# mLSTM normalisers carried as rows, state stores on the scalar queue, and the RWKV inverse's masks in fp16 on VectorE

## The chip, the cores and the metric

The kernel runs on one core of one Trainium2 chip. The time is what the device takes for one execution, in microseconds (us). Before the change three executions took 1936.51 us in the median (1935.79 to 1941.13).

## The reference, cut to what matters

One inference step of a two-layer hybrid network on 384 tokens: 128 context tokens and 256 latent ones, model width 1024. Layer 0 mixes with Mamba-2 SSD heads beside 16 RWKV-7 heads, layer 1 with 4 GLA heads beside 4 mLSTM heads; each layer ends in a squared-ReLU MLP. Every mixer scans the tokens in both directions, starts the latent scan from a given state and returns the context's final state. Two pieces matter here. The RWKV-7 scan is, per head and direction,

```
S_t = S_{t-1} (diag(w_t) - kk_t (kk_t * a_t)^T) + v_t k_t^T,   y_t = S_t r_t
```

and the mLSTM scan keeps beside its matrix C (128 x 256 per head and direction) a normaliser n, a vector of 128:

```
C_t = f_t C_{t-1} + i_t v_t k_t^T,   n_t = f_t n_{t-1} + i_t k_t
h_t = (C_t q_t) / max(|n_t . q_t|, exp(-m_t))
```

Inputs hold n as `state_mlstm_n` (2 directions x 4 heads x 128), outputs return it as `new_mn` in the same shape.

## The kernel before, in words

The work runs through four parts: the mixer of layer 0 ("ab"), its MLP, the mixer of layer 1 ("cd"), its MLP. All big products take a weight from memory (`raw`), split it into a high part `wH` (ScalarE, L265) and a low part `wL` (mostly VectorE, L223), and multiply three times on TensorE (`dps`). In the two mixers these products are the filler beside the scans. Python generators give the steps of each scan and of the filler, `run` takes them in turn by step counts, and the tile framework's scheduler then fixes one static order for each engine. Each engine works through its list in order, so an instruction that waits holds all behind it.

**The RWKV inverse** (`rw_inverse`, from L1210). The scan goes in chunks of 64 tokens; a strictly triangular matrix A per head and chunk (six chunks, two heads on the two halves of the partitions, in `Q`) has to be inverted. There are 16 such inverses, one per pair of heads and direction, one in each round of part "ab". An inverse starts from a mask of A for blocks of 1 (`AO`), and then doubles the block size in five levels, m = 2 to 32: a masked copy of A (`AOb`, block diagonal over the two heads, two buffers) meets the inverse so far (`pz`), the product is copied to `Zb` by ScalarE, two more products (`pw2`, `pt2`) update `W` and `Tm` on VectorE. Before, the masked copies of the five levels are made by GpSimd straight from `Q` (fp32) and a bf16 mask, one multiplication for each head's half. ScalarE also writes `AHb`, an fp16 copy of A in the same block-diagonal layout; its off-diagonal blocks were set to zero once. It is used at the end of the inverse only, together with the rest `ALb`.

**mLSTM** (`ml_core`, from L2268; one call per head, spread over two rounds of part "cd"). It loads C and n of both directions side by side into `CN` (n is column 256), one DMA for C and one of 128 x 1 elements per direction for n. The context's final state is a product of 257 columns in PSUM, copied to `mso` by ScalarE, and stored by two DMAs from SyncE's queue, 128 x 256 for C (L2307) and 128 x 1 for n (L2308). SyncE's queue (SP) also issues every weight load. `gla_core` stores its final states the same way (L2208), and `cd_setup` the stabiliser `new_mm` (L2091).

Of the kernel before, what the change touches and what calls it, by code (L numbers as in the profile page):

```python
# [8 lines left out]
F32 = mybir.dt.float32  # L9
F32R = mybir.dt.float32r  # L10
BF16 = mybir.dt.bfloat16
F16 = mybir.dt.float16
U32 = mybir.dt.uint32
AF = mybir.ActivationFunctionType
ALU = mybir.AluOpType
# [148 lines left out]
class Net:  # L164
# [793 lines left out]
    def rw_setup(self):  # L958
        nc = self.nc
        rp = self.rp  # L960
        i64 = rp.tile([128, 64], F16, name="i64h")
        nc.vector.tensor_copy(i64, self.c("i64"))
        self.i64h = i64
        self.i128h = rp.tile([128, 128], F16, name="i128h")
        nc.vector.tensor_copy(self.i128h, self.c("ident"))
        a, b = GOFF["rw"]
        nm = COFF["r64"][1]
        self.rwmask = rp.tile([128, nm], BF16, name="rwmask")
        self.r64 = rp.tile([128, b - a - nm], F32, name="r64")
        with self.tc.tile_pool(name="rwc", bufs=1) as pp:  # L970
            t = pp.tile([128, nm], F32, name="rwc")
            nc.sync.dma_start(out=t, in_=self.I["const"][:, a:a + nm])
            nc.vector.tensor_copy(self.rwmask, t)
        nc.sync.dma_start(out=self.r64, in_=self.I["const"][:, a + nm:b])
        self.pads = []
        for i in range(1):
            t = rp.tile([128, 387], F32, name="rpad%d" % i)
            nc.gpsimd.memset(t, 0.0)
            self.pads.append(t)
        self.npad = 0  # L980
        self.mu_om = rp.tile([128, 27], F32, name="mu_om")
        self.mu_h = rp.tile([128, 27], F32, name="mu_h")
        self.ts(self.mu_om, self.par("rwkv_mu"), -1.0, ALU.mult, 1.0, ALU.add)
        self.ts(self.mu_h, self.par("rwkv_mu"), 0.5, ALU.mult)
        self.hw0 = rp.tile([128, 16], F32, name="hw0")
        self.ha0 = rp.tile([128, 16], F32, name="ha0")
        self.ts(self.hw0, self.par("rwkv_w0"), -1.0, ALU.mult)
        self.ts(self.ha0, self.par("rwkv_a0"), -1.0, ALU.mult)

        self.bks = rp.tile([128, 2, 2, 8], F32, name="bks")  # L990
        for e, h in enumerate((slice(0, 64), slice(64, 128))):
            nc.gpsimd.memset(self.bks[h, e, 0], 1.0)
            nc.gpsimd.memset(self.bks[h, e, 1], 0.0)
            ka = self.par("rwkv_k_a")[h]
            nc.vector.tensor_copy(self.bks[h, 1 - e, 0], ka)
            self.ts(self.bks[h, 1 - e, 1], ka, -1.0, ALU.mult, 1.0, ALU.add)
        self.wdt = rp.tile([128, T], F32, name="wdt")
        self.adt = rp.tile([128, T], F32, name="adt")
        self.gdt = rp.tile([128, T], F32, name="gdt")
# [208 lines left out]
    def rw_inverse(self, d, st):  # L1208

        nc = self.nc
        rp = self.rpi
        dn = "fb"[d]
        halves = (slice(0, 64), slice(64, 128))
        A = [st["Q"][h, e, :, 0, :] for e, h in enumerate(halves)]
        i64 = self.c("i64")
        f = lambda ap: ap.rearrange("p c t -> p (c t)")  # L1220
        b6 = lambda ap: ap.unsqueeze(1).to_broadcast([ap.shape[0], 6, 64])
        h6 = lambda nm, bufs: rp.tile([128, 6, 64], F16, tag=nm, name=nm, bufs=bufs)

        def heads(name, lhs, rhs):
            p = self.psi(name)
            for c in range(6):
                for h in halves:
                    self.mm(p[h, 64 * c:64 * c + 64], lhs[h, c, :] if lhs.shape[1] == 6 else lhs[h, :],
                            rhs[h, c, :] if rhs.shape[1] == 6 else rhs[h, :])
            return p[:, :T]  # L1230

        def pairs(name, lhs, rhs):
            p = self.psi(name)
            for c in range(6):
                self.mm(p[:, 64 * c:64 * c + 64], lhs[:, c, :], rhs[:, c, :])
            return p[:, :T]

        AO = h6("AO", 1)
        for h, a in zip(halves, A):
            self.tt(AO[h], a, b6(self.rm("rwl1_" + dn)[h]), ALU.mult)  # L1240
        W = h6("W", 2)
        self.tt(W, b6(i64), AO, ALU.subtract)
        yield
        pt = heads("pt", W, self.i64h)
        Tm = h6("T", 2)
        self.acopy(f(Tm), pt)
        for h, a in zip(halves, A):
            self.acopy(self.AHb[h, :, h], a)
        yield
        for n, m in enumerate((2, 4, 8, 16, 32)):  # L1250
            AOb = self.AOb[n % 2]
            for h, a in zip(halves, A):
                self.tt(AOb[h, :, h], a, b6(self.rm("rwl%d_%s" % (m, dn))[h]), ALU.mult, eng=nc.gpsimd)
            pz = pairs("pz", AOb, Tm)
            Zb = self.Zb
            zv = pz.rearrange("p (c t) -> p c t", c=6)
            for h in halves:
                self.acopy(Zb[h, :, h], zv[h])
            yield
            if m < 32:  # L1260
                pw = pairs("pw2", Zb, W)
            pt = self.psi("pt2")
            for c in range(6):
                for h in halves:
                    self.mm(pt[h, 64 * c:64 * c + 64], W[h, c, :], Zb[h, c, h])
            T2 = h6("T", 2)
            if m < 32:
                W2 = h6("W", 2)
                self.tt(f(W2), f(W), pw, ALU.subtract)
                W = W2  # L1270
            self.tt(f(T2), f(Tm), pt[:, :T], ALU.subtract)
            Tm = T2
            if n == 0:
                for h, a in zip(halves, A):
                    self.tt(self.ALb[h, :, h], a, self.AHb[h, :, h], ALU.subtract)
            yield

        pe = self.psi("pe")
        self.mm(pe[:, :T], self.i128h, f(Tm), stop=False)
        for c in range(6):  # L1280
            self.mm(pe[:, 64 * c:64 * c + 64], self.AHb[:, c, :], Tm[:, c, :], start=False, stop=False)
            self.mm(pe[:, 64 * c:64 * c + 64], self.ALb[:, c, :], Tm[:, c, :], start=False, stop=c == 5)
        pt = heads("pt", Tm, self.i64h)
        E = h6("AO", 1)
        self.tt(E, b6(i64), pe[:, :T].rearrange("p (c t) -> p c t", c=6), ALU.subtract)
        W = h6("W", 2)
        self.acopy(f(W), pt)
        yield
        pc = heads("pc", E, W)
        WF = self.rpc.tile([128, 6, 64], F32, tag="WF", name="WF", bufs=2)  # L1290
        self.tt(f(WF), f(W), pc, ALU.add)
        yield
        st["W"] = WF
# [698 lines left out]
    def cd_setup(self, es, hs):  # L1992
# [25 lines left out]
        for d in range(2):  # L2018
            nc.sync.dma_start(out=gbias[32 * d:32 * d + 4, :], in_=I["mlstm_i_b"][0, d].rearrange("(h o) -> h o", o=1))
            nc.sync.dma_start(out=gbias[64 + 32 * d:68 + 32 * d, :], in_=I["mlstm_f_b"][0, d].rearrange("(h o) -> h o", o=1))  # L2020
            nc.sync.dma_start(out=m0[32 * d:32 * d + 4, :], in_=I["state_mlstm_m"][0, 0, d].rearrange("(h o) -> h o", o=1))
        self.Ms = p.tile([128, T], F32R, name="Ms")
        self.ct = p.tile([128, 3, 64], F32, name="mct")
        self.emt = p.tile([128, 3, 64], F32, name="memt")
        self.wit = p.tile([128, 2, 64], F32, name="mwit")
# [4 lines left out]
        def evac(ps):  # L2030
# [57 lines left out]
                V.tensor_copy(f(self.wit), p2[:, 0:128])  # L2088
                self.ts(self.wst, p2[:, 128:192], 128.0 ** -0.5, ALU.mult)
            for d in range(2):  # L2090
                nc.sync.dma_start(out=self.O["new_mm"][0, 0, d].rearrange("(h o) -> h o", o=1), in_=self.mfin[32 * d:32 * d + 4, :])  # L2091
        second = self.dense_cm(W, 0, hs, evac, placed=(6176, 4, 32))
        return [first, second]

# [23 lines left out]
    def gla_core(self, h, u, ys):  # L2118
# [72 lines left out]
        for i, (n, d) in enumerate(((0, 0), (0, 1), (1, 0), (2, 1))):  # L2191
# [13 lines left out]
            if n == 0:  # L2205
                so = tl("gso", [128, 256], 2)
                self.acopy(so, ps[:, :256])
                nc.sync.dma_start(out=self.O["new_gla"][0, 0, d, h], in_=so)  # L2208
            else:
                self.stt(S1[:, d], S0[:, d], gl[:, d:d + 1], ps[:, :256], ALU.mult, ALU.add)  # L2210
            yield
# [60 lines left out]
    def ml_core(self, h, u, ys):  # L2272
# [7 lines left out]
        tks = [slice(128 * n, 128 * n + 128) for n in range(3)]  # L2280
        CN = tl("CN", [128, 2, 257])
        nc.sync.dma_start(out=CN[:, :, 0:256], in_=self.I["state_mlstm_c"][0, 0, :, h].rearrange("d k v -> k d v"))
        for d in range(2):
            nc.sync.dma_start(out=CN[:, d, 256:257], in_=self.I["state_mlstm_n"][0, 0, d, h].rearrange("(k o) -> k o", o=1))

        Gs = tl("Gs", [128, 5, 128])
        blocks = ((1, 2), (0, 0), (1, 1), (2, 2), (2, 1))
# [12 lines left out]
        for d in range(2):  # L2300
            kw = tl("kw", [128, 128], 2)
            self.act(kw, pt[:, :128], AF.Copy, scale=self.wst[:, 32 * d + h:32 * d + h + 1])
            ps = u["ps"]()
            self.mm(ps[:, :257], kw, v[:, 0])
            so = tl("mso", [128, 257], 2)
            self.acopy(so, ps[:, :257])
            nc.sync.dma_start(out=self.O["new_mc"][0, 0, d, h], in_=so[:, 0:256])  # L2307
            nc.sync.dma_start(out=self.O["new_mn"][0, 0, d, h].rearrange("(k o) -> k o", o=1), in_=so[:, 256:257])  # L2308
            yield
        for d in range(2):  # L2310
            r = 32 * d + h
# [161 lines left out]
```

## Time and profile before

| | |
|---|---|
| median of three executions | 1936.51 us |
| the profiled execution | 1942.11 us |
| its span, first to last instruction | 1940.0 us |
| TensorE busy | 1811.7 us (93%) |
| VectorE busy | 1346.5 us (69%) |
| ScalarE busy | 1062.5 us (55%) |
| GpSimd busy | 413.0 us (21%) |
| mean granted TensorE clock | 0.953 of full |

PE stands for TensorE, PEld for its weight loads, DVE for VectorE, ACT for ScalarE, POOL for GpSimd, SP for SyncE; a q behind a name is that engine's instruction queue. A busy time is the union of the instructions' spans. A waiting time is put down to what ended it last. The granted clock is the share of full speed that the chip allowed TensorE in a stretch. Part "ab" lies from about 60 to 980 us in the span, its 16 inverses from 122 to 850 us; part "cd" runs from 1200 to 1660 us, its rounds of heads from 1256 to 1620 us.

### The profile page before, as it was taken

To read this page: it belongs to the slowest core of one execution; us is meant where nothing else is said; L and a number is where in the kernel's file an instruction comes from. 1 tells how busy PE (TensorE), PEld (TensorE's weight loads), DVE (VectorE), ACT (ScalarE), POOL (GpSimd) and SP (SyncE) were. 2 spreads that over 40 slices of the span, in tenths; PEclk is the share of its full clock that TensorE was granted. 3 is DMA by queue.
4 is the path that set the end of the run, shared out by engine and by line. 5 is a ranking of instruction groups with operands and counts; after the bars stand their busy time and mean duration, and the time that the engine had idled before them with its cause. 6 is when DMAs were issued, how large, how long until landed. Compare 5 with 4: busy or idle time off the path is not lost.

```text
span 1940.0 us, 37528 instructions
## 1 busy us (share of the span) xinstructions
PE 1811.7 (93%) x13651; PEld 1510.4 (78%) x13651; DVE 1346.5 (69%) x2890; ACT 1062.5 (55%) x2670; POOL 413.0 (21%) x455
## 2 busy tenths in 40 slices
PE   7879998999999999999899999899998988899998
PEld 3676666766666676876899998598988888799887
DVE  3696788888787886767766334675976867766434
ACT  3557464746564666544555332476776756555322
POOL 2244323242434143421100002011201112200000
PEclk9889999999899897999999999799999999899999
DMA  8422343333333322336344643344434234244432
GB/s 268 119 73 71 102 128 91 97 94 116 96 106 117 86 52 64 91 118 180 87 120 127 204 129 92 102 114 88 94 98 90 80 87 125 87 120 128 146 129 87
DMA packets 322525, 213.57 MB, mean 110 GB/s; under 512 B 41936, under 2 KB 307958, under 8 KB 322340
## 3 DMA queue, kind: packets, MB, share of 16 engines
q1 hardware_dynamic: 319508, 210.45, 38.6%
q8 instruction: 107, 1.75, 0.4%
q10 hardware_dynamic: 2480, 0.59, 0.2%
q14 instruction: 78, 0.64, 0.1%
q0 software_dynamic: 352, 0.13, 0.0%
HBM read 201.32 MB, written 9.78 MB: 109 GB/s over the span
## 4 chain that ended last, share of the span: by engine, by line
PE 70%; DVE 14%; DMA 6%; ACT 5%; issue 3%; POOL 1%; SPq 1%; DVEq 0%; ACTq 0%; POOLq 0%
PE dps L209 43%; PE o L209 7%; PE ps L209 4%; PE mod L209 3%; DVE wL L223 3%; PE aux L209 2%; DMA raw<-in_w_in_cd 2%; DVE cacc L230 2%; PE psc L209 2%; DMA raw<-in_w_mod 1%; PE py L209 1%; PE pt L209 1%; PE pr L209 1%; ACT wH L265 1%; PE pu L209 1%
## 5 line engine op out<-in xcount | busy, mean ns | idle before, releaser
L265 ACT ACTIVATE wH<-raw 128x256 fp32r<-128x256 f32 (+1 forms) x788 | 363.6, 481 | 477.3 <-PE dps L209 344.3
L223 DVE TENSOR_TENSOR wL<-raw,wH 128x256 fp32r<-128x256 f32 (+2 forms) x769 | 424.6, 570 | 270.8 <-ACT wH L265 262.6
L223 POOL TENSOR_TENSOR AO<-Q,rwmask 64x384 f16<-64x384 f32 x160 | 164.4, 1031 | 257.7 <-PE pz L209 185.4
L265 ACT ACTIVATE Zb<-pz 64x384 f16<-64x384 f32 x160 | 77.2, 483 | 41.0 <-PE pz L209 38.5
L230 DVE SCALAR_TENSOR_TENSOR cacc<-rows,params,cacc 128x192 f32<-128x192 f32 (+1 forms) x192 | 96.5, 504 | 0.8
L209 PE MATMUL dps<-sH,wH 128*128 128x384 f32 x232 | 87.7, 379 | 4.9 <-DVE m L223 4.4
L209 PE MATMUL dps<-sH,wL 128*128 128x384 f32 x232 | 81.6, 352 | 0.4 <-DVE wL L223 0.3
L209 PE MATMUL dps<-sL,wH 128*128 128x384 f32 x232 | 81.5, 352 | 0.3 <-DVE sL L223 0.3
L209 PE MATMUL dps<-h0H,wH 128*128 128x384 f32 (+2 forms) x150 | 61.4, 413 | 18.4 <-ACT h0H L233 7.8
L223 POOL TENSOR_TENSOR gDb<-gb 128x384 f32<-128x384 f32 x28 | 32.1, 1147 | 149.4 <-DVE gb L2145 81.0
L209 PE MATMUL mod<-xT,cond 128*32 128x384 f32 (+1 forms) x320 | 55.5, 514 | 8.4 <-DVE Q L223 3.7
L209 PE MATMUL dps<-h0L,wH 128*128 128x384 f32 (+2 forms) x150 | 55.5, 370 | 3.5 <-DVE h0L L230 3.5
L209 PE MATMUL dps<-h6H,wH 128*128 128x384 f32 (+2 forms) x150 | 56.0, 375 | 2.9 <-ACT wH L265 2.7
L209 PE MATMUL dps<-h4H,wH 128*128 128x384 f32 (+2 forms) x150 | 56.2, 380 | 2.1 <-ACT h4H L233 2.1
L209 PE MATMUL dps<-h2H,wH 128*128 128x384 f32 (+2 forms) x150 | 58.1, 387 | 0.0
L209 PEld LDWEIGHTS dps<-h0H,wH 128*128 128x128 f32 (+1 forms) x150 | 29.1, 196 | 33.9 <-ACT h0H L233 9.4
L209 PE MATMUL dps<-h1L,wH 128*128 128x384 f32 (+2 forms) x150 | 55.2, 368 | 0.0
L209 PE MATMUL dps<-h0H,wL 128*128 128x384 f32 (+2 forms) x150 | 55.1, 367 | 0.0
L209 PE MATMUL dps<-h1H,wH 128*128 128x384 f32 (+2 forms) x150 | 54.1, 362 | 0.0
L209 PE MATMUL dps<-h1H,wL 128*128 128x384 f32 (+2 forms) x150 | 53.7, 358 | 0.0
L209 PEld LDWEIGHTS dps<-sH,wH 128*128 128x128 f32 x232 | 45.3, 195 | 10.0 <-issue 5.1
L209 PE MATMUL dps<-h2L,wH 128*128 128x384 f32 (+2 forms) x150 | 53.0, 353 | 0.0
(1112 smaller groups left out, 5614.3 us busy)
## 6 DMA issues: line engine op xcount, KB each, us to landing
raw<-in_w_mlp_up SPq DMA_DIRECT2D x64, 512.0 KB
raw<-in_w_mlp_down SPq DMA_DIRECT2D x64, 512.0 KB
raw<-in_w_in_ab SPq DMA_DIRECT2D x204, 128.0 KB
xT<-in_w_mod SPq DMA_DIRECT2D x128, 192.0 KB
raw<-in_w_in_cd SPq DMA_DIRECT2D x192, 128.0 KB
raw<-in_w_mod SPq DMA_DIRECT2D x64, 192.0 KB
raw<-in_w_mod SPq DMA_DIRECT2D x32, 256.0 KB
raw<-in_w_out_cd SPq DMA_DIRECT2D x64, 128.0 KB
```

What stands on the lines that cost most here:

```text
L209: self.nc.tensor.matmul(out, lhsT, rhs, start=start, stop=stop)
L223: (eng or self.nc.vector).tensor_tensor(out=out, in0=a, in1=b, op=op)
L230: self.nc.vector.scalar_tensor_tensor(out=out, in0=a, scalar=s, in1=b, op0=op0, op1=op1)
L265: self.nc.scalar.activation(out=out, in_=in_, func=AF.Copy)
```

## The change

Three things are changed.

In the inverse the mask tile becomes fp16. ScalarE's copy `AHb` moves to the start, and the masks are applied to it: a VectorE multiplication per half for `AO`, and one VectorE multiplication over all 128 partitions and both heads' columns (768 elements) for each level, `off(n)`. The zero blocks of `AHb` keep the result block diagonal. Masks for levels 0 and 1 are made ahead of the first level, the others two levels ahead.

The normalisers are loaded once, as 8 rows of 128, in `cd_setup`, turned by one TensorE transposition and kept in `mn`; `ml_core` copies its column into `CN` on VectorE. The final ones are gathered in `mno` by VectorE, turned once after the last head, copied and stored as 8 rows. `mso` shrinks by a column, and the last head's `ml_core` has one step more.

The stores of final states in part "cd" (`new_mm`, `new_gla`, `new_mc`, `new_mn`) go out from ScalarE's queue.

```diff
-        self.rwmask = rp.tile([128, nm], BF16, name="rwmask")
+        self.rwmask = rp.tile([128, nm], F16, name="rwmask")
...
+        for h, a in zip(halves, A):
+            self.acopy(self.AHb[h, :, h], a)
+
+        def off(n):
+
+            two = lambda ap: ap.rearrange("p c (e t) -> p c e t", e=2)
+            self.tt(two(self.AOb[n % 2]), two(self.AHb),
+                    self.rm("rwl%d_%s" % (2 << n, dn)).unsqueeze(1).unsqueeze(1).to_broadcast([128, 6, 2, 64]), ALU.mult)
         AO = h6("AO", 1)
-        for h, a in zip(halves, A):
-            self.tt(AO[h], a, b6(self.rm("rwl1_" + dn)[h]), ALU.mult)
+        for h in halves:
+            self.tt(AO[h], self.AHb[h, :, h], b6(self.rm("rwl1_" + dn)[h]), ALU.mult)
         W = h6("W", 2)
         self.tt(W, b6(i64), AO, ALU.subtract)
+        off(0)
         yield
...
-        for h, a in zip(halves, A):
-            self.acopy(self.AHb[h, :, h], a)
+        off(1)
         yield
         for n, m in enumerate((2, 4, 8, 16, 32)):
-            AOb = self.AOb[n % 2]
-            for h, a in zip(halves, A):
-                self.tt(AOb[h, :, h], a, b6(self.rm("rwl%d_%s" % (m, dn))[h]), ALU.mult, eng=nc.gpsimd)
-            pz = pairs("pz", AOb, Tm)
+            pz = pairs("pz", self.AOb[n % 2], Tm)
...
             Tm = T2
+            if n < 3:
+                off(n + 2)
...
+        self.mn = p.tile([128, 2, 4], F32, name="mn")
+        self.mno = p.tile([128, 2, 4], F32, name="mno")
+        t = self.mpool.tile([128, T], F32, tag="nt", name="mnr", bufs=2)[0:8, 0:128]
+        nc.sync.dma_start(out=t, in_=I["state_mlstm_n"][0, 0].rearrange("d h k -> (d h) k"))
+        pn = self.psp("mn")
+        self.tr(pn[:, 0:8], t)
+        V.tensor_copy(self.mn.rearrange("p d h -> p (d h)"), pn[:, 0:8])
...
-                nc.sync.dma_start(out=self.O["new_mm"][0, 0, d].rearrange("(h o) -> h o", o=1), in_=self.mfin[32 * d:32 * d + 4, :])
+                nc.scalar.dma_start(out=self.O["new_mm"][0, 0, d].rearrange("(h o) -> h o", o=1), in_=self.mfin[32 * d:32 * d + 4, :])
...
-                nc.sync.dma_start(out=self.O["new_gla"][0, 0, d, h], in_=so)
+                nc.scalar.dma_start(out=self.O["new_gla"][0, 0, d, h], in_=so)
...
-        for d in range(2):
-            nc.sync.dma_start(out=CN[:, d, 256:257], in_=self.I["state_mlstm_n"][0, 0, d, h].rearrange("(k o) -> k o", o=1))
+        V.tensor_copy(CN[:, :, 256], self.mn[:, :, h])
...
-            so = tl("mso", [128, 257], 2)
-            self.acopy(so, ps[:, :257])
-            nc.sync.dma_start(out=self.O["new_mc"][0, 0, d, h], in_=so[:, 0:256])
-            nc.sync.dma_start(out=self.O["new_mn"][0, 0, d, h].rearrange("(k o) -> k o", o=1), in_=so[:, 256:257])
+            so = tl("mso", [128, 256], 2)
+            self.acopy(so, ps[:, :256])
+            V.tensor_copy(self.mno[:, d, h:h + 1], ps[:, 256:257])
+            nc.scalar.dma_start(out=self.O["new_mc"][0, 0, d, h], in_=so)
+            yield
+        if h == 3:
+            pt = u["ps"]()
+            self.tr(pt[0:8, 0:128], self.mno.rearrange("p d h -> p (d h)"))
+            so = tl("mso", [128, 256], 2)[0:8, 0:128]
+            self.acopy(so, pt[0:8, 0:128])
+            nc.scalar.dma_start(out=self.O["new_mn"][0, 0].rearrange("d h k -> (d h) k"), in_=so)
             yield
```

How the change moves instructions is seen at three places. The first is VectorE's list at the start of the second inverse, before:

```order
L223 TENSOR_TENSOR AO<-Q,rwmask 64x384 x2
L223 TENSOR_TENSOR ALb<-Q,AHb 64x6x64
L223 TENSOR_TENSOR W<-const_base,AO 128x384
L1123 SCALAR_TENSOR_TENSOR b<-r_759,lw 128x384
L227 TENSOR_SCALAR UV<-pu 64x2x64
L223 TENSOR_TENSOR lw<-b,lw 128x384
```

and the same place now:

```order
L223 TENSOR_TENSOR AO<-AHb,rwmask 64x384 x2
L223 TENSOR_TENSOR AO_793<-AHb,rwmask 128x768
L223 TENSOR_TENSOR W<-const_base,AO 128x384
L223 TENSOR_TENSOR AO_795<-AHb,rwmask 128x768
L223 TENSOR_TENSOR ALb<-Q,AHb 64x6x64
L227 TENSOR_SCALAR UV<-pu 64x2x64
L1123 SCALAR_TENSOR_TENSOR b<-r_759,lw 128x384
L223 TENSOR_TENSOR lw<-b,lw 128x384
```

AO_793 and AO_795 are the two buffers `AOb`. Every inverse has five such new instructions, and the first of its masks reads ScalarE's copy where it read VectorE's own `Q`.

The second place is SyncE's list where the first mLSTM head's final state is stored, before:

```order
L664 DMA raw<-in_w_in_cd 128x256 x8
L2307 DMA out_new_mc<-mso 128x256
L2308 DMA out_new_mn<-mso 128x1
L664 DMA raw<-in_w_in_cd 128x2x128 x3
L2307 DMA out_new_mc<-mso 128x256
L2308 DMA out_new_mn<-mso 128x1
L664 DMA raw<-in_w_in_cd 128x2x128 x8
L2208 DMA out_new_gla<-gso 128x256
```

In the changed kernel only the weight loads are left there, and ScalarE's list at that place reads:

```order
L265 ACTIVATE mso<-ps 128x256
L265 ACTIVATE wH<-raw 128x256
L2322 DMA out_new_mc<-mso 128x256
L233 ACTIVATE kw<-ps,mwst 128x128
L265 ACTIVATE wH<-raw 128x256
L233 ACTIVATE gE<-gDf 128x96x2 x2
```

The C store follows its copy by one instruction, and the n store is gone from all lists until the last head.

The third place is ScalarE's list at the start of part "cd", between the MLP's residual and the first normalised tile h0H, before:

```order
L233 ACTIVATE rr<-rr 128x384
L265 ACTIVATE wH<-raw 128x256 x2
L233 ACTIVATE r_16437<-sx,const_base 128x384
L233 ACTIVATE r_16437<-r_16437 128x384
L233 ACTIVATE h0H<-nh,modv_105 128x128
L233 ACTIVATE h0H<-nh,modv_105 128x256
```

and now:

```order
L233 ACTIVATE rr<-rr 128x384
L265 ACTIVATE wH<-raw 128x256 x2
L265 ACTIVATE modsb<-mod 128x384
L233 ACTIVATE r_16364<-sx,const_base 128x384
L233 ACTIVATE r_16364<-r_16364 128x384
L265 ACTIVATE wH<-raw 128x256
L233 ACTIVATE h0H<-nh,modv_105 128x128
```

`modsb` is the copy of the last modulation product `mod`, which reads weights from memory; before it stood behind h5H. On VectorE and TensorE the modulation's end has moved ahead in the same way (TensorE: all 32 pieces of `mod`, then the new transposition `mn`, then the first `dps`).

## Rows read from the trace of the kernel before

**Rows 1.** The page: the chain that ended last, by engine, shares of the span.

```profile
PE 70%; DVE 14%; DMA 6%; ACT 5%; issue 3%; POOL 1%; SPq 1%; DVEq 0%; ACTq 0%; POOLq 0%
```

**Rows 2.** Windows by stage: length, busy us (instructions) per engine, PEclk, DMA share, GB/s.

```profile
122.00:850.00 728.00, 680.95 (x7286) 496.22 (x7286) 585.21 (x1288) 428.13 (x1087) 263.82 (x266) 0.94 0.33 93
1243.00:1625.00 382.00, 358.51 (x2178) 336.71 (x2178) 278.56 (x627) 252.39 (x733) 50.00 (x66) 0.97 0.41 94
```

**Rows 3.** Windows around the four mLSTM heads' stores, and two others; columns as above.

```profile
1325.00:1335.00 10.00, 6.91 (x39) 6.27 (x38) 1.77 (x5) 3.80 (x13) 0.92 (x2) 0.88 0.61 92
1405.00:1415.00 10.00, 8.34 (x55) 7.52 (x54) 2.60 (x7) 5.00 (x17) 0.92 (x2) 1.00 0.62 97
1485.00:1495.00 10.00, 7.64 (x54) 7.08 (x53) 3.08 (x7) 4.68 (x16) 0.91 (x2) 1.00 0.67 97
1560.00:1575.00 15.00, 10.18 (x52) 9.17 (x52) 8.88 (x19) 7.18 (x23) 1.00 (x2) 0.89 0.51 83
1335.00:1340.00 5.00, 5.00 (x25) 4.51 (x25) 1.93 (x5) 2.33 (x7) 0.00 (x0) 0.91 0.33 87
1576.00:1620.00 44.00, 44.00 (x249) 42.68 (x249) 24.59 (x66) 24.68 (x67) 3.15 (x16) 1.00 0.35 102
```

**Rows 4.** Timeline of SP's queue, 1316 to 1336: start, us, line, operation, count.

```profile
1318.60 0.36 SPq L2307 DMA_DIRECT2D out_new_mc<-mso  x1
1319.01 0.42 SPq L2308 DMA_DIRECT2D out_new_mn<-mso  x1
1319.52 12.44 SPq L664 DMA_DIRECT2D raw<-in_w_in_cd  x8
...
1334.75 0.36 SPq L2208 DMA_DIRECT2D out_new_gla<-gso  x1
```

**Rows 5.** Waits of ACT, 1316 to 1336, then 1555 to 1575: total, times, longest.

```profile
ACT wH L265 <- DMA raw<-in_w_in_cd: 6.1, 2, 5.0
...
ACT wH L265 <- DMA raw<-in_w_out_cd: 5.9, 3, 4.3
```

**Rows 6.** Operations of one tile: count, min/median/max ns, first and last start.

```profile
L1370 ACTq DMA_DIRECT2D out_new_rwkv<-fo x16: 602/635/742, 183.0 to 882.5; - x16
L265 ACT ACTIVATE AHb<-Q x32: 507/521/525, 122.5 to 822.0; 64x384 f16<-64x384 f32 x32
L223 DVE TENSOR_TENSOR BK<-BK,b x16: 941/952/1667, 111.8 to 783.3; 128x768 f32<-128x768 f32 x16
```

**Rows 7.** Groups by form, POOL then DVE, 122 to 850: busy us, mean ns, idle before.

```profile
L223 POOL TENSOR_TENSOR AO<-Q,rwmask 64x384 f16<-64x384 f32 x160 | 164.4, 1031 | 257.7 <-PE pz L209 185.4 <-DVE Q L223 62.7 <-DVE wL L223 2.6
L223 DVE TENSOR_TENSOR wL<-raw,wH 128x256 fp32r<-128x256 f32 x187 | 111.5, 601 | 37.3 <-ACT wH L265 31.7 <-issue 4.0 <-PE dps L209 0.6
L223 DVE TENSOR_TENSOR T<-T,pt 128x384 f16<-128x384 f16 x78 | 42.5, 545 | 2.5 <-PE pt L209 2.5
L223 DVE TENSOR_TENSOR BK<-BK,b 128x768 f32<-128x768 f32 x15 | 16.9, 1128 | 1.7 <-POOL BK L223 1.7
```

**Rows 8.** The group of `wL` on DVE, 1243 to 1625.

```profile
L223 DVE TENSOR_TENSOR wL<-raw,wH 128x256 fp32r<-128x256 f32 x243 | 110.3, 461 | 66.0 <-ACT wH L265 63.9 <-PE dps L209 0.9 <-ACT gso L265 0.3
```

**Rows 9.** Start of part "cd": a window, timeline rows, and the last `dps` row.

```profile
1208.00:1219.00 11.00, 6.26 (x44) 1.57 (x36) 11.00 (x21) 3.94 (x9) 5.93 (x7) 0.88 0.69 220
...
1212.19 0.55 DVE L223 TENSOR_TENSOR sx<-sx,t 128x384 f32<-128x384 f32 x1
...
1212.77 0.61 ACT L233 ACTIVATE r<-sx,const_base 128x384 f32<-128x384 f32 x1 [8.01 <-DVE sx L223]
1215.32 0.40 ACT L233 ACTIVATE h0H<-nh,modv 128x128 fp32r<-128x128 f32 x1 [1.37 <-DVE nh L230]
1229.96 0.49 ACT L265 ACTIVATE modsb<-mod 128x384 f32<-128x384 f32 x1 [6.20 <-PE mod L209]
1232.04 0.52 ACT L265 ACTIVATE h7H<-nh 128x384 fp32r<-128x384 f32 x1
...
L209 PE MATMUL dps<-h7H,wL x2: 343/393/443, 1233.4 to 1241.4; 128*64 128x384 f32 x1, 128*128 128x384 f32 x1
```

## The prediction

> **What bounds the kernel now.** I read the chain of waits first: TensorE makes 70% of it, VectorE 14%, transfers 6%, ScalarE 5% and GpSimd 1% [rows 1]. So a microsecond taken from VectorE, ScalarE or GpSimd shows only where TensorE waits for it. Then the windows by stage [rows 2]: in the stage of the inverses TensorE idles 728.00 - 680.95 = 47 us, VectorE is busy 585 of 728 (143 idle) and GpSimd 264; in the rounds of "cd" TensorE idles 382.00 - 358.51 = 23.5 us while ScalarE has 130 us free and VectorE 103. The reader should see that neither stage has much to give: all that this change could win without shortening TensorE's own work is about 70 us of idle time, and what the granted clock gives back beside it (0.94 and 0.97 of full in the two stages).
>
> Third, smaller windows [rows 3]. Half of the 23.5 us lies in four short pieces, at the four mLSTM heads' stores: (10 - 6.91) + (10 - 8.34) + (10 - 7.64) + (15 - 10.18) = 11.9 us. There the DMA share is 0.51 to 0.67 while only 83 to 97 GB/s are moved. The window behind the first of them moves 87 GB/s at a share of 0.33, with a 128 KB GLA store issued at 1334.75 [rows 4] and TensorE busy throughout; a later stretch moves 102 GB/s at 0.35, and TensorE does 249 matmuls in 44 us without a hole [rows 3]. So in the four pieces something occupies the DMA engines without moving bytes. SP's queue shows the candidate [rows 4]: behind the n store of 128 pieces of 4 bytes, eight weight issues take 12.4 us. And ScalarE waits for `raw` in two of the pieces, 6.1 and 5.9 us, once 5.0 at a stretch [rows 5]: the weight queue is late, then the split, then the product.
>
> **The change part by part.** Sums are made against the profiled execution, 1942.1 us; the median of the runs shown is 5.6 us lower, and I take that off at the end.
>
> *Stores in "cd": -13 us.* The n stores of 128 x 1 go; one store of 8 rows remains after the last head. The C stores stay, on another queue. If the holes belong to the n stores, TensorE gets back 11.9 us, and the clock of 0.88 and 0.89 in the first and fourth piece gives 0.12 x 10 + 0.11 x 15 = 2.9 us more: 14.8 us in all. Zero is the other end: the C stores may have made the holes. I take 13, since the GLA store of the same 128 KB leaves TensorE full in the next window, but one such window can't clear eight C stores quite. What is late next there is the split of the weights itself, which at 1576 to 1620 keeps TensorE full [rows 3]. The n loads of 128 x 1 go as well; I count nothing for them, since these windows, with the holes, are the stage's larger losses already.
>
> *Issues on ScalarE: +1 us.* 19 stores move to ScalarE's queue (2 `new_mm`, 8 `new_gla`, 8 `new_mc`, 1 `new_mn`). ScalarE's own issues of this kind take 0.635 us [rows 6]: 12 us out of its 130 free. Queued behind such an issue stands the next `wH`, for which VectorE's `wL` and the product wait; the filler has several pieces in hand, so most of it hides: 0 to +4, taken as +1. SP loses the same issues, which brings weights forward by 0.36 and 0.42 us a head [rows 4]. The copies of n (12 on VectorE, a transposition, one ScalarE copy) are 0.2 to 0.6 us each and off the path; if VectorE's idle 103 us did not cover them they would cost 3.
>
> *Start of "cd": -2 us.* The modulation's end (`modsb`, `modv`, `moda`) now stands ahead of `sx`, `r` and h0H, which so wait for the last modulation weights. Those are due at about 1219: the window to 1219 moves 220 GB/s x 11 us = 2.42 MB [rows 9], and the last twelve pieces of 192 KB are 2.36 MB. Then `modsb` to the instruction behind `moda` 2.1 us (1229.96 to 1232.04), three `t` and `sx` at 0.55 = 2.2, `r` to h0H 2.55 (1212.77 to 1215.32): h0H at 1225.9 instead of 1215.3. That is a new wait of 10.6 us on ScalarE and VectorE; queued behind it is all of the normalisation, and TensorE waits for it. But TensorE then has no `mod` left and two dense panels at once. Lower end: 48 matmuls at 44/249 = 0.177 us, 8.5 us, done at 1234.4. Upper end: the normalisation keeps its 17.2 us from h0H to the end of h7H, done a microsecond after it at 1244.1. Before, the second panel ended at 1241.8 [rows 9]. So -7 to +2; the middle is -2.6, and I take -2. The load of `mnr` and its transposition are needed only behind these weights and hide there.
>
> *Masks, GpSimd's side.* 160 operations of 1.031 us go, 164.4 us or 62% of GpSimd's time in the stage [rows 7]. VectorE's operations with two SBUF inputs are slower beside GpSimd: `wL` takes 0.601 us in this stage [rows 7] and 0.461 in "cd" [rows 8], where GpSimd is busy 50 of 382 us, while `T<-T,pt`, with a PSUM input, shows a plain 0.545. For `wL` alone the excess is 187 x 0.14 = 26 us; if all of VectorE's 585 us had the same excess, 0.14/0.601 = 23%, it would be 136. 62% of these is 16 to 84 us of VectorE time given back; I take the middle, 50.
>
> *Masks, VectorE's side.* 80 new operations of 128 x 768 in fp16; `AO` stays 32 operations of the same size. No operation of this form, with two 16-bit SBUF inputs, is in the trace. By bytes it is like the fp32 one of 384 elements, 0.545 us; by elements like `BK<-BK,b` of 768, 0.952 in the median [rows 6], or 0.952 x 0.601/0.461 = 1.24 beside a busy GpSimd. The nearest rows are 0.545 and 0.952, and I take 0.75 between them: 60 us (44 to 99). VectorE thus gains 10 us of work net (-40 to +83), of 143 idle. At its 14% of the chain that is +1 us.
>
> *Masks, waits.* `AO` and off(0) now wait for ScalarE's two AHb copies (0.521 us each [rows 6]) at the start of each of the 16 inverses; before, `AO` started from VectorE's own `Q`. Behind that wait on VectorE stand `W`, off(1), `ALb`, `UV` and the next scan `b`, and TensorE's pz behind those. TensorE has filler there, so I count nothing, but up to 1.5 us a round if the filler's `wL` is itself behind the wait. Against it, GpSimd's remaining 106 operations no longer queue behind pairs of masks, and VectorE's waits on them (1.7 us at `BK` alone [rows 7], perhaps twice that in all) shrink. I take -3 for this; the stage as a whole: -2 us (-15 to +27).
>
> The Trainium skill, "VectorE: DVE Perf Modes", section "The perf-mode tier table (the rule you actually need)", says that a tensor_tensor on 16-bit SBUF data runs at twice the rate of fp32. No run here shows it; it is a rival below, as the lower of my two rows.
>
> A rule that speaks against the change is in the Trainium skill, "Trainium Kernel Development and Optimization", section "Key Constraints": transfers issued from SP, ScalarE and GpSimd share the same 16 DMA engines and interleave, and more queues save only issue time. By it the queue's move alone is worth the 0.36 us an issue, and if the holes belong to the C stores they stay; the trace's low GB/s at a high DMA share speaks for the 4-byte pieces, and does not prove it.
>
> Sum: -13 + 1 - 2 - 2 = -16: 1942.1 - 16 = 1926 in a profiled execution, 1920 as a median.
>
> **The rivals.**
>
> *The masks run at the rate of bytes.* 80 x 0.545 = 44 us against 50 given back: VectorE loses 6 us, up to 40. It has priority where TensorE waits, and I put the stage at -7 instead of -2: 1942.1 - 21 - 5.6 = 1915. For it: T and W of 384 elements take 0.54 whether fp16 or fp32, so only size and source show. Against: nothing in the trace shows any 16-bit gain.
>
> *The holes stay.* The C stores, not the n stores, fill the DMA engines, or another wait takes their place at once: ScalarE's splits with the new issues among them. Then -2 + 1 - 2 = -3: 1933. For it: both stores go out within 0.8 us [rows 4], so the trace can't part them. Against: the GLA control and the low GB/s.
>
> *Slower.* VectorE becomes the bound of the inverse: masks at 1.24 us (99 us) with only 16 given back, so +83 us, 5.2 a round, and 1.5 more of waiting for AHb: 6.7 of its 8.9 idle us a round. It decides from about 4 us a round, where VectorE is behind when the inverse's next level asks for it. Of 16 x 6.7 = 107 us I let a quarter reach TensorE, 27: -13 + 1 - 2 + 27 = +13, 1949. For it: VectorE is 80% busy here already and GpSimd, idle for 64% of the stage, loses work to it. Against: the levels have other rows' work between them, and the masks are made two levels ahead.
>
> **How the numbers follow.** Chances: the forecast 0.44 (its own range 1911 to 1930), masks at the rate of bytes 0.28 (1905 to 1922), holes stay 0.15 (1929 to 1940), slower 0.13 (1940 to 1960). A measurement of this kernel can tell about 0.3%, 5.8 us, from no change: faster is below 1930.7, slower above 1942.3. The first two cases lie below: 0.72. The third is the same: 0.15. The fourth is slower: 0.13. The range that leaves out two in ten cuts the slower case beyond 1941 and the best ends below 1900: 1900 to 1941.
>
> **What would show it.** In the windows around the last copies of `mso`, TensorE full at a DMA share near 0.35, and no ScalarE wait for `raw` there; if the share stays over 0.5 the holes were the C stores'. The mask rows on VectorE: 0.55, 0.95, or more. `wL` in the stage of the inverses falling from 0.601 towards 0.461, GpSimd's busy time in the page near 413 - 164 = 250. h0H about 10 us later against `sx`'s old place while the first panels end no later. ScalarE's new issues near 0.635. I am wrong if TensorE's idle time in the inverse stage grows past its 47 us, if the holes stay behind the C stores, or if the start of "cd" loses the ten microseconds that its first tile does.

## The result

The changed kernel takes 1877.11 us in the median of four executions (1874.27 to 1879.82), against 1938.82 for the kernel before on the same chip: a ratio of 0.9674, 95% interval 0.9637 to 0.9711. That is 62 us faster. The prediction said 1920, with a range of 1900 to 1941, so the time lies 23 us below the range.

The chain of waits by engine, from the page of the kernel after:

```profile
PE 74%; DVE 10%; ACT 7%; issue 4%; DMA 3%; POOL 1%; SPq 1%; ACTq 0%; DVEq 0%; POOLq 0%
```

Against [rows 1] VectorE has gone from 14% to 10% and the transfers from 6% to 3%. Where the time went is read by following the same matmuls: the `dps` at the end of part "ab" start 48 us earlier than before, those at the first mLSTM store 49 us earlier, those behind the last rounds 65 us. So 48 us come from the inverses, nothing from the setup of "cd", and 16 from its rounds.

The stage of the inverses ends at 852.3 us before and 802.7 after (each 1.5 us ahead of the last copy `Zb`). Windows over it, before and then after (length; busy us and instructions of PE, PEld, DVE, ACT, POOL; granted clock; DMA share; GB/s):

```profile
122.00:852.30 730.30, 683.25 (x7313) 498.06 (x7313) 586.74 (x1292) 428.55 (x1088) 264.55 (x267) 0.93 0.33 93
```

```profile
122.00:802.70 680.70, 656.02 (x7299) 479.63 (x7298) 550.36 (x1364) 427.69 (x1086) 99.46 (x106) 0.98 0.35 98
```

The stage is 49.6 us shorter. TensorE's idle time fell from 47.1 to 24.7 us, its busy time from 683 to 656 us for the same matmuls. The second part goes with the granted clock, in three digits 0.935 before and 0.977 after: over the whole stretch, idle time included, 0.065 of 730 is 48 us lost to the lower clock, 0.023 of 681 is 15. VectorE is 36 us less busy although it took over the masks. Its groups by form there, of the kernel after (busy us, mean ns, idle before):

```profile
L223 DVE TENSOR_TENSOR wL<-raw,wH 128x256 fp32r<-128x256 f32 x187 | 86.0, 465 | 25.0 <-ACT wH L265 23.6 <-ACT lw L233 0.7 <-issue 0.4
L223 DVE TENSOR_TENSOR AO<-AHb,rwmask 128x768 f16<-128x768 f16 x80 | 48.9, 612 | 7.0 <-PE pz L209 6.0 <-ACT AHb L265 0.6
...
L223 DVE TENSOR_TENSOR AO<-AHb,rwmask 64x384 f16<-64x384 f16 x32 | 11.2, 349 | 0.7
```

and a group of the same view of the kernel before, of 122 to 850 us:

```profile
L223 DVE TENSOR_TENSOR AO<-Q,rwmask 64x384 f16<-64x384 f32 x32 | 21.8, 681 | 0.4
```

`wL` fell from 601 ns [rows 7] to 465 in the mean, about the value that it had in "cd" [rows 8]. The new masks took 612 ns in the mean, and the median of all operations that write AO from AHb is 549. `AO` itself became faster, 681 to 349 in the mean (555 to 349 in the median). VectorE waited 0.6 us for ScalarE's AHb in all. Without the masks, VectorE was busy 586.7 - 21.8 = 565 us before and 550.4 - 48.9 - 11.2 = 490 after: 75 us came back from operations that the change doesn't touch, for 165 us that GpSimd no longer works.

These means hide what happened to single operations. All `wL` of the stage, before and then after (count; min, median and max ns; first and last start):

```profile
L223 DVE TENSOR_TENSOR wL<-raw,wH x187: 400/420/2048, 128.4 to 847.9; 128x256 fp32r<-128x256 f32 x187
```

```profile
L223 DVE TENSOR_TENSOR wL<-raw,wH x187: 389/417/2074, 126.7 to 800.9; 128x256 fp32r<-128x256 f32 x187
```

The median has not moved. What moved is the number of long ones: 47 of 187 took over 1.3 times the median before, 12 after. In each of these 59 a GpSimd instruction was already running when `wL` began, and `wL` ended 275 to 287 ns after that instruction did. No `wL` that met no GpSimd instruction took more than 427 ns, before or after. Three rows of the timeline of the kernel before show a held `wL` and a free one:

```profile
322.27 1.12 POOL L223 TENSOR_TENSOR AO<-Q,rwmask 64x384 f16<-64x384 f32 x1
322.54 1.14 DVE L223 TENSOR_TENSOR wL<-raw,wH 128x256 fp32r<-128x256 f32 x1
...
323.80 0.41 DVE L223 TENSOR_TENSOR wL<-raw,wH 128x256 fp32r<-128x256 f32 x1
```

So VectorE did not run at a lower rate beside GpSimd here. Some of its operations were held until a GpSimd instruction that began earlier had ended. Counting all of VectorE's operations in the stage that took over a quarter (and over 80 ns) longer than the median of their kind without a GpSimd instruction beside it, there are 151 before and 39 after, and all of them met one. The time above that median, summed over all operations that met one, is 97 us before and 31 after. `T<-T,pt`, with one input in PSUM, was not held before: 556 ns at most, though 29 of its 79 met a GpSimd instruction.

In "cd", the windows that answer to [rows 3], around the stores of the four mLSTM heads:

```profile
1275.00:1285.00 10.00, 10.00 (x66) 9.21 (x66) 4.07 (x10) 5.97 (x19) 0.92 (x2) 1.00 0.46 117
1356.00:1366.00 10.00, 10.00 (x53) 9.16 (x53) 4.74 (x11) 6.84 (x22) 0.46 (x1) 1.00 0.43 106
1435.00:1445.00 10.00, 10.00 (x54) 9.23 (x54) 4.74 (x11) 6.86 (x21) 0.46 (x1) 1.00 0.42 106
1500.00:1518.00 18.00, 17.49 (x106) 16.57 (x106) 13.22 (x30) 12.07 (x38) 3.15 (x3) 1.00 0.48 140
```

The holes are gone but for 0.5 us in the last window, at more GB/s with a smaller DMA share. The start of "cd", timeline of the kernel after:

```profile
1171.87 0.49 ACT L265 ACTIVATE modsb<-mod 128x384 f32<-128x384 f32 x1 [14.80 <-PE mod L209]
...
1178.58 0.40 ACT L233 ACTIVATE h0H<-nh,modv 128x128 fp32r<-128x128 f32 x1 [0.94 <-DVE nh L230]
...
1189.38 0.51 ACT L265 ACTIVATE h7H<-nh 128x384 fp32r<-128x384 f32 x1
```

ScalarE waits 14.8 us for the last `mod`. Shifted by the 48 us of "ab", h0H comes at 1226.6, where the prediction had 1225.9, and the path from h0H to the end of h7H shrank from 17.2 to 11.3 us.

### The profile page after: what moved, and what is told of

Read it like the earlier page. It is cut to its first block, busy times and chain, and to the rows that moved or that the text cites. A ratio compares the mean times of both kernels' runs of the same rounds, so it can differ in the third digit from the quotient of the medians.

```text
span 1874.9 us, 37380 instructions
## 1 busy us (share of the span) xinstructions
PE 1775.9 (95%) x13653; PEld 1486.6 (79%) x13653; DVE 1314.0 (70%) x2983; ACT 1064.5 (57%) x2671; POOL 251.0 (13%) x295
## 4 chain that ended last, share of the span: by engine, by line
PE 74%; DVE 10%; ACT 7%; issue 4%; DMA 3%; POOL 1%; SPq 1%; ACTq 0%; DVEq 0%; POOLq 0%
PE dps L209 45%; PE o L209 7%; PE ps L209 4%; PE mod L209 3%; PE aux L209 2%; PE psc L209 2%; DVE wL L223 2%; PE py L209 1%; PE pt L209 1%; DVE cacc L230 1%; PE pr L209 1%; PE pw L209 1%; ACT wH L265 1%; ACT Zb L265 1%; PE ms L209 1%
## 5 line engine op out<-in xcount | busy, mean ns | idle before, releaser
L223 DVE TENSOR_TENSOR wL<-raw,wH 128x256 fp32r<-128x256 f32 (+2 forms) x769 | 397.2, 534 | 240.6 <-ACT wH L265 236.9
L223 DVE TENSOR_TENSOR AO<-AHb,rwmask 128x768 f16<-128x768 f16 (+1 forms) x112 | 60.1, 537 | 7.7 <-PE pz L209 6.0
L223 POOL TENSOR_TENSOR BK<-BK,kkk 128x768 f32<-128x768 f32 x16 | 33.8, 2112 | 221.9 <-DVE BK L227 108.1
L209 PE MATMUL dps<-h6H,wL 128*128 128x384 f32 (+2 forms) x150 | 51.8, 345 | 1.1 <-DVE wL L223 1.1
L209 PE MATMUL dps<-h2H,wL 128*128 128x384 f32 (+2 forms) x150 | 52.2, 348 | 0.0
```

What stands on the lines that cost most here:

```text
L209: self.nc.tensor.matmul(out, lhsT, rhs, start=start, stop=stop)
L223: (eng or self.nc.vector).tensor_tensor(out=out, in0=a, in1=b, op=op)
```

## The experiments

Ratios are to the kernel before on the same chip, intervals 95%. The median of the kernel before was 1938.82, 1943.49, 1939.67 and 1942.85 us in the four sets of runs, so a difference in us between runs of two sets is good to about 5 us. One theory in two halves runs through the expectations: that GpSimd's masks cost VectorE's time, and that VectorE's time in this stage reaches the end.

**The inverse alone.** The mask tile and `rw_inverse`, nothing in "cd".

> Only the inverse's part of the change: masks on VectorE from the fp16 copy AHb; part "cd" as before. The traces of before and after differ by 47.5 us over the stage of the inverses (the last blocks of pz start 47.5 us sooner) and by 17 us in "cd". Theory 1 (the inverse's part by itself gives the larger gain, because GpSimd's masks slowed VectorE): about 1938 - 47 = 1891. Theory 2 (the two parts lean on each other, or the order written for the whole program changed): another number, 1905 or more. In the trace wL in the stage of the inverses should be near 0.465 us, as in the changed kernel (0.601 before).

Measured 1898.63 us, ratio 0.9772 (0.9733 to 0.9811), 45 us faster. The window of the stage:

```profile
122.00:802.20 680.20, 656.28 (x7303) 480.75 (x7304) 551.45 (x1366) 427.93 (x1087) 99.35 (x106) 0.98 0.35 98
```

It is that of the changed kernel to half a microsecond, and `wL` takes 471 ns in the mean. Theory 1 stands, 8 us above its number.

**"cd" alone.** The other pieces of the diff.

> Only the part "cd" of the change: normalisers as rows, stores from ScalarE; the inverse as before, masks on GpSimd. Theory 1 (the parts add): about 1938 - 17 = 1921, with wL in the inverse stage still at 0.60. My prediction's own terms for this part, -13 + 1 - 2, say 1924. Theory 2 (this part also changes the inverse's stage by its new static order): outside 1915 to 1927.

Measured 1922.62 us, ratio 0.9893 (0.9859 to 0.9928): 21 us faster, `wL` at 605 ns in the stage of the inverses. 45 and 21 make 66, where both together gave 62 to 66: the parts add. The stage of the inverses, which this run does not touch, is 722 us long in its trace and 727 in that of "the queue alone", against 730 before: the length of a stage in one trace is good to some 8 us.

**GpSimd busy again, for nothing.** In each level, beside VectorE's fast masks, and with a sixth cleared tile `ghost`:

```diff
+            for h in halves:
+                self.tt(self.ghost[h, :, h], A[h.start // 64], Tm[h], ALU.mult, eng=nc.gpsimd)
             pz = pairs("pz", self.AOb[n % 2], Tm)
```

> The changed kernel, and beside it 160 extra GpSimd multiplications of the old form (64 x 384, fp32 and fp16 in, fp16 out) into a tile that nobody reads, two in each level, taking Q and the inverse so far. VectorE keeps its fast masks. Theory 1 (sharing with GpSimd is what the masks cost: VectorE's operations with two SBUF inputs are slower beside it, TensorE gets holes, its clock falls): most of the 47 us come back, 1910 to 1925, wL in the stage near 0.60 and the granted clock near 0.94 to 0.95. Theory 2 (the gain is in the masks' own latency, or in the new static order): the time stays at 1877 to 1885, whatever wL does.

Measured 1941.24 us, ratio 0.9985 (0.9963 to 1.0007): the whole gain of the change is lost, that of "cd" included, more than expected.

```profile
122.00:871.30 749.30, 686.19 (x7292) 497.24 (x7287) 630.21 (x1364) 428.18 (x1085) 263.95 (x264) 0.93 0.32 89
```

VectorE, with the same 1364 instructions as in the changed kernel, is 80 us busier, TensorE's idle time is 63 us and the clock 0.93. The masks cost 701 ns instead of 612 and `wL` 546, less than the 0.60 expected of it. By the profile no VectorE instruction waited for a ghost; what grew is the number of held ones, 170 in place of 39, with 116 us above the median in place of 31.

**The same waits, hardly any work.** The ghost over 2 columns instead of 64:

```diff
-                self.tt(self.ghost[h, :, h], A[h.start // 64], Tm[h], ALU.mult, eng=nc.gpsimd)
+                self.tt(self.ghost[h, :, h.start:h.start + 2], A[h.start // 64][:, :, 0:2], Tm[h, :, 0:2], ALU.mult, eng=nc.gpsimd)
```

> The kernel with 160 extra GpSimd multiplications again, with the same inputs, order and waits, but each over 2 columns of each chunk (64 x 6 x 2 in place of 64 x 6 x 64), so that GpSimd is hardly busy with them. Theory 1 (in that run the time GpSimd was busy beside VectorE was the cost): near the changed kernel, 1877 to 1890, wL back at 0.465. Theory 2 (its cost was the new waits, of VectorE's T on GpSimd's reading and of GpSimd's other work behind T): most of the 64 us stay, over 1915.

Measured 1878.99 us, ratio 0.9691 (0.9655 to 0.9726): that of the changed kernel, with `wL` at 473 ns. The ghosts are there (GpSimd's rows of the tile; count, then min, median and max ns), and the window of the stage is nearly that of the changed kernel:

```profile
L223 POOL TENSOR_TENSOR GH<-Q,T x160: 207/282/2060, 131.8 to 806.9; 64x12 f16<-64x12 f32 x160
```

```profile
122.00:805.60 683.60, 657.36 (x7299) 479.89 (x7299) 553.35 (x1366) 427.78 (x1087) 156.19 (x264) 0.97 0.35 98
```

So it is not the waits, nor GpSimd's queue, nor a static order that has 160 more instructions. It is not GpSimd's busy time as such either: GpSimd is 57 us busier than in the changed kernel, where the expectation had it hardly busy, and VectorE only 3 us. 379 VectorE operations met a GpSimd one, against 195 in the changed kernel, but 41 were held for long, against 39. What costs is long GpSimd instructions beside VectorE, about 1 us each in the other run and 0.28 here.

**Every mask twice on VectorE.**

```diff
-            self.tt(two(self.AOb[n % 2]), two(self.AHb),
+            for _ in range(2):
+                self.tt(two(self.AOb[n % 2]), two(self.AHb),
```

> The changed kernel with each of the 80 masks of 128 x 768 made twice on VectorE: 78 or 80 more operations, about 43 us more work at 0.55 us each, no more on GpSimd. Theory 1 (what counts is how much longer VectorE's work takes, and 45 to 65 us of it were given back when GpSimd's masks went): 43 us of new VectorE work should cost a large share of the 47 us, 20 to 40: 1897 to 1917. Theory 2 (VectorE has room, the loss beside GpSimd comes at the wrong places, or not through VectorE's total at all): 0 to 10 us, 1877 to 1887.

Measured 1916.31 us, ratio 0.9854 (0.9813 to 0.9896), 39 us above the changed kernel (35 by the ratios), inside the range of theory 1.

```profile
122.00:839.90 717.90, 681.00 (x7290) 494.32 (x7291) 590.18 (x1444) 427.89 (x1084) 104.03 (x106) 0.94 0.33 93
```

40 us more of VectorE, with GpSimd nearly as idle as in the changed kernel, make the stage 37 us longer: 12 of them idle time of TensorE, the other 25 longer busy time for the same matmuls, at a clock of 0.94 for 0.98. VectorE still has 128 us of idle time.

**No masks.** `off(n)` returns at once in all inverses but the first; 15 inverses run on masks left in the buffers.

> The changed kernel, but the 80 masks of 128 x 768 are made in the first inverse alone; the other 15 inverses use what then stands in the two buffers, so 75 masks (46 us of VectorE work at 0.612) are left out on any engine. It shows what the masks still cost. Theory 1 (VectorE's work in this stage reaches the end nearly one to one, as the doubled masks showed, 39 us for 43 of work): 1877 - 40 = 1837. Theory 1b (the same, but TensorE has only 25 us of idle time and 14 us of clock left in the stage, so it flattens): 1850 to 1862. Theory 2 (only more VectorE work hurts, the masks as they are lie in its idle time): 1870 to 1880.

Measured 1866.45 us, ratio 0.9626 (0.9595 to 0.9657), 11 us below the changed kernel (9 by the ratios).

```profile
122.00:793.80 671.80, 651.46 (x7296) 477.66 (x7294) 515.82 (x1291) 426.66 (x1086) 98.27 (x107) 0.98 0.36 101
```

35 us less of VectorE give 9 us. Both forms of theory 1 asked for more, and theory 2, which began at 1870, for less: the curve that is steep above the changed kernel is nearly flat below it.

**Masks on VectorE, made the old way**, from fp32 Q, one operation for each half.

```diff
-            self.tt(two(self.AOb[n % 2]), two(self.AHb),
-                    self.rm("rwl%d_%s" % (2 << n, dn)).unsqueeze(1).unsqueeze(1).to_broadcast([128, 6, 2, 64]), ALU.mult)
+            for h, a in zip(halves, A):
+                self.tt(self.AOb[n % 2][h, :, h], a, b6(self.rm("rwl%d_%s" % (2 << n, dn))[h]), ALU.mult)
```

`AO` is made from `a` again, too.

> The changed kernel with the masks on VectorE, but made as GpSimd made them, from fp32 Q and one operation for each half: 160 of 64 x 384 at about 0.555 us each in place of 80 at 0.612, and AO from Q again (0.555 in place of 0.349): 89 - 49 + 7 = 47 us more VectorE work, no GpSimd masks. Theory 1 (VectorE's work counts at about 0.9 us a us): 1877 + 42 = 1919, so moving the masks off GpSimd alone would win next to nothing (the cd part alone gave 1923), and fp16 with one operation a level is what makes the change pay. Theory 2 (freeing GpSimd is the gain, the masks' form is secondary): 1877 to 1895.

Measured 1908.4 us, ratio 0.9842 (0.9812 to 0.9872): 31 us of the gain are lost (33 by the ratios).

```profile
122.00:833.80 711.80, 673.47 (x7305) 488.75 (x7304) 610.44 (x1447) 426.79 (x1086) 104.30 (x106) 0.96 0.33 94
```

60 us of VectorE make 31 us. Between the two theories, nearer the first: leaving GpSimd gives 10 to 14 us (0.9842 against the 0.9893 of "cd" alone, on another chip), fp16 with one operation a level the other 31 to 33. The type and the number of operations were not tried apart.

**More work from VectorE to ScalarE.** `kkk`, `BK` and `kk` of the preparation as activations.

```diff
-        self.ts(kk, k, self.par("rwkv_k_k", j), ALU.mult)
+        self.act(kk, k, AF.Copy, scale=self.par("rwkv_k_k", j))
...
-            self.ts(BK[:, :, i, :], six(ta), self.bks[:, i, 0, j:j + 1], ALU.mult, self.bks[:, i, 1, j:j + 1], ALU.add)
+            self.act(BK[:, :, i, :], six(ta), AF.Identity, bias=self.bks[:, i, 1, j:j + 1], scale=self.bks[:, i, 0, j:j + 1])
```

> The changed kernel with three more groups moved from VectorE to ScalarE in the RWKV preparation: the copy of k into kkk (64 x 384, 0.350 us), the scaling of ta into BK (0.471) and the scaling of k into kk (0.44): 14, 30 and 7 of them in the stage, 22 us off VectorE, about as much on ScalarE, which has 253 us free there. Theory 1 (VectorE's work reaches the end at about 0.9): 1877 - 18 = 1859, faster than both kernels. Theory 2 (ScalarE's splits wH come late instead, or there is no more to give): 1872 to 1890.

Measured 1884.4 us, ratio 0.9701 (0.9658 to 0.9744), no gain, inside the range of theory 2. VectorE's busy time fell by 13 us only and ScalarE's rose by 27; below the changed kernel there is little to have, as the run without masks shows.

**The queue alone**, on the kernel before: `nc.sync` becomes `nc.scalar` at the four stores, the n stores stay 128 x 1.

> The kernel before with only the queue changed: new_mm, new_gla, new_mc and the 8 stores of n (still 128 x 1, 4 bytes a piece) go out from ScalarE. Theory 1 (the pieces of 4 bytes fill the DMA engines, whatever queue issues them): holes and DMA share over 0.5 behind the stores stay, 1930 to 1945 against 1941 of before. Theory 2 (the stores block the weight queue itself; another queue frees it): 1920 to 1928, the holes gone.

Measured 1947.12 us, ratio 1.0026 (1.0006 to 1.0046): nothing gained, if anything 5 us lost. Two windows behind the stores of the third head, the deepest of the four holes:

```profile
1485.00:1495.00 10.00, 4.78 (x38) 4.33 (x36) 2.17 (x5) 3.07 (x10) 0.46 (x1) 0.87 0.97 101
1490.00:1500.00 10.00, 4.96 (x17) 4.74 (x18) 1.70 (x4) 4.26 (x14) 0.46 (x1) 0.66 0.54 98
```

The holes are there, at a DMA share up to 0.97 with 101 GB/s.

**The rows alone**, on the changed kernel: the same four stores back on `nc.sync`.

> The changed kernel with only the queue put back: rows of n, but all stores of states from SP's queue. Theory 1 (pieces of 4 bytes): nothing lost, 1874 to 1884. Theory 2 (the queue): part of the 20 us that the cd part gave comes back, 1888 to 1900, with ScalarE waiting for raw behind the C stores.

Measured 1876.58 us, ratio 0.9647 (0.962 to 0.9674); the changed kernel beside it:

> The changed kernel once more, beside the two others on one chip, so that a few us can be told: 1874 to 1882, ratio to before 0.964 to 0.971.

Measured 1876.73 us, ratio 0.9666 (0.9642 to 0.9691). The queue is worth nothing; the gain in "cd" is that of the rows. The whole set of traces agrees: from the last `Zb` to the end of the span, the three kernels with n as 128 x 1 take 1086 to 1092 us, the ten with rows 1068 to 1077. The rows replaced loads as well as stores, and no run parts the two. But in the 12 us behind the loads of C for the second, third and fourth head TensorE idled 0.7, 2.6 and 2.5 us before and 0.7, 2.6 and 2.6 after, so those loads gave nothing; the first head's, beside the changed start of "cd", are not told apart.

## Why the prediction was wrong, by its steps

*The stores* were right in mechanism and small in size: -13 forecast, 16 between the traces, 21 for the part alone. The holes belonged to the 4-byte pieces; the two queue runs settle what the trace of before could not part. The rule of the Trainium skill ("Trainium Kernel Development and Optimization", section "Key Constraints") that was weighed there, on the queue's move alone, agrees with the queue runs: 1.0026 for the move, 0.9647 against 0.9666 for its undoing.

*The issues on ScalarE* (+1) are within what the queue runs can tell; an issue of `new_mc` took 0.34 us in the median, where 0.635 was put. *The start of "cd"* (-2) measured about 0; h0H came within 0.7 us of where it was put, and the path behind it took 11.3 us, below the 17.2 us of the upper bound.

*The masks on GpSimd's side.* Given back were 75 us, forecast 50 in bounds of 16 to 84. That GpSimd's masks cost VectorE time was forecast, and the ghosts show it: 165 us of GpSimd's work cost VectorE 75 to 80 us, in both directions. The form was not the forecast one: the prediction spread an excess of 0.14 us over all `wL` and over VectorE's 585 us, where 47 of 187 `wL` and 151 of all 1292 operations were held, until a GpSimd instruction ended, and the rest lost nothing.

*The masks on VectorE's side.* 49 us, forecast 60 in bounds of 44 to 99. The median near 0.549 is the lower row, by bytes. The tier table of the Trainium skill ("VectorE: DVE Perf Modes", "The perf-mode tier table (the rule you actually need)"), whose column is for bf16, agrees with this fp16 row: 768 elements in 549 ns, where `KR<-r,eI`, 384 elements in fp32, takes 548. The mean of 612 lies above it by five held ones (to 2183 ns). That `AO` would win too, 10.6 us, was not counted. Together VectorE is 36 us less busy, where the forecast had 10 more.

*The step that failed* is what a microsecond of VectorE is worth: "At its 14% of the chain that is +1 us". With the measured -36 the same rule would still have said -5; the stage became 50 us shorter. The other runs show 37 us for 40 (masks twice), 31 for 60 (the old form), 69 for 80 (ghosts), but 9 for 35 below the changed kernel. An average share over the whole kernel does not price a stage in which VectorE is 80% busy. And the prediction left out the second half of the price: in these windows the granted clock is lower where TensorE idles more, from 0.98 at 20 to 25 us idle (no masks, changed) to 0.96 at 38 (old form), 0.94 at 37 (masks twice), 0.93 at 47 and 63 (before, ghosts). Idle time plus the loss by the clock, (1 - clock) x length with the clock in three digits, is 34, 40, 69, 80, 95 and 116 us in these six; taken from their lengths it leaves 633 to 643 us in each. So the "about 70 us of idle time" that the prediction named as all there was to win left the clock beside it as a remark, when TensorE's busy time at the higher clock was the larger half here, 27 us to 22 of idle time.

The rival "masks run at the rate of bytes" had the right mask and the same wrong exchange rate: 1915. The slower rival, too, set the price by the stage, a quarter of VectorE's added time, but had VectorE's balance the wrong way round: up to 83 us more, where 36 less were measured.

What stays open: VectorE's busy time does not order the runs alone. Before, 587 us with GpSimd at 265 make 730 us; masks twice, 590 with GpSimd at 104, make 718; the old form, 610 with 104, makes 712. The two runs that keep the old inverse have 722 and 727 us, so against masks twice the difference is within what traces of one stage differ by; against the old form, 10 to 18 us, it is not. Held time goes along with it, 97 us before and 37 and 40 in the other two. That a held microsecond costs TensorE more than one of even work is a reading, and was not tried. That the masks on GpSimd came late is not the reason as far as the trace shows: TensorE waited under 2 us in all for `AO` and `AOb` in the kernel before. That the clock falls because of the idle time is read from the runs as well. It does not follow it strictly: masks twice and the old form idle alike, 37 and 38 us, at 0.941 and 0.957.

## What to carry to other kernels

Work that GpSimd does "for free" is paid by VectorE where both run: here about 0.45 us for each microsecond of instructions of 1 us, so 2.06 us of mask on GpSimd cost more VectorE time than the same mask made on VectorE in fp16 at 0.55 to 0.61. GpSimd instructions of 0.28 us cost next to nothing. When a mean is high, look at the median and the longest first: a few held operations and a lower rate look the same in a mean. In a stage where an engine beside TensorE is four fifths busy, price its time by that stage and add the clock, not by its share of the chain; and expect the gain to flatten once TensorE's idle time is small. Turn columns of single numbers into rows before they go to memory; which queue issues the store mattered nothing.

## What the runs showed that was not expected

The price of GpSimd's work is paid by few operations on VectorE. `KR`, two fp32 inputs of 384 elements, took 791 ns in the mean before and 548 after, with medians of 553 and 547: five of its 14 were held before, none after. With the masks made the old way on VectorE its mean is 782, though GpSimd is as idle as in masks twice, because two were held, up to 2170 ns. Which operations meet a GpSimd instruction is set by the static order, so such a mean can come back without more work on GpSimd.

Half-partition multiplications of 64 x 384 ran in 349 ns with both inputs in fp16, against a median of 555 with one of them in fp32 and 521 for ScalarE's copy of the same shape [rows 6].
